# Convolution taps in a two-block transformer kernel: ScalarE's tap products added by accumulating DMA transfers in place of Pool additions

## The chip, the cores and the metric

The kernel runs on one core of a Trainium2 chip. The metric is the time of one execution on the device in microseconds (us). The engines are called PE (TensorE, matrix products; PEld are its weight loads), DVE (VectorE), ACT (ScalarE), POOL (GpSimd) and SP (SyncE, which issues the transfers between DRAM and the on-chip memory SBUF). Each engine works through its own queue of instructions in order and waits on semaphores for the others.

## The reference

The input is a sequence of 1024 tokens with 1024 features. Two blocks follow one another. The first has three branches (a recurrent one of RWKV type, a convolution and an attention to a memory of 256 rows) that are gated, added, projected and added to the input. The second has two layers with gated scans and differential attention. The change lies in the convolution of the first block:

```
u = glu_in[..., :1024] * sigmoid(glu_in[..., 1024:])
u = conv_general_dilated(u, w_dw[:, None, :], (1,), [(30, 0)],
        feature_group_count=1024) + b_dw        # 31 taps per feature, causal
u = silu(layernorm(u)) * silu(conv_gate)
y_conv = u @ w_proj_conv + b_proj_conv
```

Each of the 1024 features has 31 weights of its own: the result at time t is the sum of `w[j] * u[t - 30 + j]` over j from 0 to 30, plus a bias.

## The kernel before, in words

Features lie on the 128 partitions, in eight tiles, and time along the rows. The convolution is done by element-wise work in 16 groups, one for each tile of features `i` and half of the time `h` (512 columns). A group is the generator `taps` (line 567 in the print below). It loads `u` with 30 columns of the past (lines 574 and 577) and shares the 31 taps out. ACT starts the accumulator `acc` with tap 0 and the bias (line 581). DVE adds taps 1 to 14 to `acc`, each by one instruction that multiplies and adds (line 589). The last 16 taps (`GT = 16`) are multiplied by ACT (line 585): the first product goes straight into a second sum, `acg`, the other 15 into a tile `ut`, of which there are two buffers, and POOL adds each to `acg` (line 587, through the helper `tt`, whose instruction has line 211 in the profile). At the end DVE adds `acg` to `acc` (line 592), and the sum is stored to DRAM as `uc` (line 593). `acc`, `acg` and `u` have one buffer each, so a group starts when the one before it has let go of them.

The groups run inside the recurrent branch (`rwkv`), beside two other kinds of work. PE's order there is the written order (`pinned`): 16 units of 24 steps, with a step of the recurrence (`unit_chain`: `S`, `Z`, `SA`), a piece of the matrices for the next unit (`unit_gram`, whose short DVE recurrence writes `B`, `tm` and `T`), some of the preparation (`unit_prep`: `AR`, `BK`), and then a burst of dense matmuls `ps` (`project`) that cover the waits of the recurrence. In two of three steps `next_tap` moves the current group of taps by one tap of ACT, one of POOL and one of DVE. The dense matmuls take weights split into a high and a low half; ACT writes the high half `whi`, and the low half `wlo` is a subtraction on DVE or, for the second four row blocks of a weight tile in this stretch (`wlo_g`), on POOL.

`keep` in `taps` ties an instruction of ACT or DVE behind the instruction that was traced before it on the same engine. All else on ACT, DVE, POOL and SP is ordered by a planner that simulates the program; the additions on POOL and the last addition of a group are not tied. Semaphores are placed by the framework: a transfer that writes `acg` waits for the last one that wrote it, and a product that writes a `ut` buffer waits for the last reader of that buffer.

Of the kernel before, what the change touches and what calls it, by code (L numbers as in the profile page):

```python
# [14 lines left out]
ALU = mybir.AluOpType  # L15
# [166 lines left out]
class Kern:  # L182
# [18 lines left out]
    def keep(self, ins):  # L201

        if self.strict:
            self.tc.keep_in_program_order(ins)
# [362 lines left out]
    def taps(self, i, h):  # L567

        nc, p1 = self.nc, self.r1
        u = p1.tile([128, 542], F32, tag="uh", name="uh")  # L570
        src = self.D[f"u{i}"]
        if h == 0:
            nc.gpsimd.memset(u[:, 0:30], 0.0)
            nc.sync.dma_start(out=u[:, 30:542], in_=src[:, 0:512])
            self.spill(f"uc{i}")
        else:
            nc.sync.dma_start(out=u, in_=src[:, 482:1024])
        keep = self.tc.keep_in_program_order
        w = lambda j: self.V("w_dw", 31 * i + j)
        acc, acg = (p1.tile([128, 512], F32, tag=t, name=t) for t in ("uacc", "uacg"))  # L580
        keep(nc.scalar.activation(out=acc, in_=u[:, 0:512], func=AF.Identity, scale=w(0), bias=self.V("b_dw", i)))  # L581
        for k in range(GT):
            j = 31 - GT + k
            t = acg if k == 0 else p1.tile([128, 512], F32, tag="ut", name="ut", bufs=2)
            keep(nc.scalar.activation(out=t, in_=u[:, j:j + 512], func=AF.Copy, scale=w(j)))  # L585
            if k:
                self.tt(acg, acg, t, ALU.add, eng=nc.gpsimd)
            if 1 <= k <= 30 - GT:
                keep(nc.vector.scalar_tensor_tensor(out=acc, in0=u[:, k:k + 512], scalar=w(k), in1=acc, op0=ALU.mult, op1=ALU.add))  # L589
            if k:  # L590
                yield False
        self.tt(acc, acc, acg, ALU.add)
        nc.sync.dma_start(out=self.D[f"uc{i}"][:, h * 512:h * 512 + 512], in_=acc)
# [1271 lines left out]
```

## Time and profile before

| | before |
|---|---|
| median of 3 runs | 3795.87 us (3791.98 to 3798.04) |
| profiled execution | 3792.68 us |
| its span, first to last instruction | 3790.8 us |
| PE busy in the span | 3511.8 us, 93% |
| DVE busy | 2309.6 us, 61% |
| ACT busy | 1847.6 us, 49% |
| POOL busy | 863.9 us, 23% |
| mean granted TensorE clock | 0.970 |

Busy time is the time in which an engine had an instruction in work; a busy PE is not PE at its peak, since its matmuls overlap. Times inside a profile count from the first instruction. An engine's idle time is put down to what ended it, as the semaphores tell it.

### The profile page before, as it was taken

How to read it: one execution, taken by the hardware profiler on the slowest of the kernel's cores; microseconds unless marked ns; L12 is line 12 of the kernel's file. 1: busy time of each engine (PE TensorE's matmuls, PEld its weight loads, DVE VectorE, ACT ScalarE, POOL GpSimd, SP SyncE). 2: the span in 40 equal slices, each digit the busy share in tenths (PEclk: the TensorE clock that was granted, in tenths of full speed). 3: DMA queues.
4: the chain of work that ended last, by engine and by line, in shares of the span. 5: the costliest groups of instructions: out<-in, count | busy, mean ns of one | idle time of the engine just before them, and what ended most of it. 6: DMA issues, size and time to landing. Idle time of an engine off the chain costs nothing.

```text
span 3790.8 us, 69648 instructions
## 1 busy us (share of the span) xinstructions
PE 3511.8 (93%) x27522; PEld 2762.9 (73%) x27522; DVE 2309.6 (61%) x4461; ACT 1847.6 (49%) x3281; POOL 863.9 (23%) x738
## 2 busy tenths in 40 slices
PE   7999999999989999999999999989899999898997
PEld 5877766766766667766778867767798667677886
DVE  4345777777777767655554463567495545774873
ACT  4333444444444444435343344575485444754762
POOL 1002333332333233343022320002222300022221
PEclk9999999999999999999999999999999999999998
DMA  4421222222222222225644444234531342344513
GB/s 146 151 91 58 89 77 75 80 80 80 80 75 83 77 83 95 76 100 184 227 156 155 138 155 149 80 118 150 168 103 56 130 146 85 115 130 149 153 42 109
DMA packets 234039, 426.09 MB, mean 112 GB/s; under 512 B 26352, under 2 KB 45808, under 8 KB 233584
## 3 DMA queue, kind: packets, MB, share of 16 engines
q1 hardware_dynamic: 233712, 421.64, 34.2%
q8 instruction: 216, 3.54, 0.4%
q14 instruction: 111, 0.91, 0.1%
HBM read 287.32 MB, written 134.22 MB: 111 GB/s over the span
## 4 chain that ended last, share of the span: by engine, by line
PE 64%; DVE 18%; DMA 6%; ACT 6%; issue 5%; POOL 1%; SPq 0%; DVEq 0%; POOLq 0%; ACTq 0%
PE ps L259 44%; PE sc L259 3%; PE o_ps L259 3%; PE tps L259 2%; PE ch L259 2%; DVE uacc L589 2%; PE g L259 1%; PE wt L262 1%; DVE tm L211 1%; DVE T L211 1%; PE aps L259 1%; DVE h L211 1%; DMA raw<-d_x 1%; DVE t L217 1%; DVE B L806 1%
## 5 line engine op out<-in xcount | busy, mean ns | idle before, releaser
L259 PE MATMUL ps<-hh,whi 128*128 128x512 f32 (+2 forms) x3056 | 1282.8, 420 | 42.7 <-DVE st L211 21.6
L259 PE MATMUL ps<-hh,wlo 128*128 128x512 f32 (+2 forms) x3056 | 1203.5, 394 | 5.2 <-DVE wlo L211 5.1
L259 PE MATMUL ps<-hl,whi 128*128 128x512 f32 (+2 forms) x3056 | 1203.3, 394 | 2.4 <-DVE hl L211 2.3
L259 PEld LDWEIGHTS ps<-hh,whi 128*128 128x128 f32 (+1 forms) x3056 | 584.3, 191 | 209.7 <-issue 29.3
L259 PEld LDWEIGHTS ps<-hh,wlo 128*128 128x128 f32 (+1 forms) x3056 | 584.3, 191 | 138.6 <-DVE wlo L211 6.6
L259 PEld LDWEIGHTS ps<-hl,whi 128*128 128x128 f32 (+1 forms) x3056 | 585.5, 192 | 128.7 <-issue 18.1
L208 ACT ACTIVATE whi<-wraw 128x512 fp32r<-128x512 f32 x486 | 303.4, 625 | 530.4 <-PE ps L259 408.6
L211 DVE TENSOR_TENSOR wlo<-wraw,whi 128x512 fp32r<-128x512 f32 x398 | 292.2, 736 | 386.2 <-ACT whi L208 346.8
L211 POOL TENSOR_TENSOR uacg<-uacg,ut 128x512 f32<-128x512 f32 x240 | 338.5, 1410 | 785.1 <-ACT ut L585 642.9
L211 POOL TENSOR_TENSOR st<-st,rope 128x512 f32<-128x512 f32 x64 | 93.4, 1480 | 892.0 <-DVE st L427 566.1
L208 ACT ACTIVATE st<-ps 128x512 f32<-128x512 f32 (+2 forms) x260 | 149.2, 574 | 214.6 <-PE ps L259 182.7
L589 DVE SCALAR_TENSOR_TENSOR uacc<-uh,vecs,uacc 128x512 f32<-128x512 f32 x224 | 207.6, 927 | 7.9 <-ACT uacc L581 6.9
L211 POOL TENSOR_TENSOR wlo<-wraw,whi 128x512 fp32r<-128x512 f32 x88 | 121.2, 1377 | 283.9 <-ACT whi L208 261.3
L211 POOL TENSOR_TENSOR acc<-acc,sq 128x512 f32<-128x512 f32 (+1 forms) x91 | 124.4, 1375 | 253.8 <-ACT sq L208 252.2
L585 ACT ACTIVATE ut<-uh,vecs 128x512 f32<-128x512 f32 x240 | 166.0, 715 | 4.4 <-POOL uacg L211 3.7
L1414 DVE TENSOR_REDUCE D<-sc 128x1 f32<-128x1024 f32 x128 | 153.9, 1219 | 13.6 <-PE sc L259 13.2
L208 ACT ACTIVATE p<-sc,D 128x1024 f32<-128x1024 f32 x128 | 142.5, 1114 | 24.5 <-DVE D L1414 23.4
L259 PE MATMUL o_ps<-h,wT 128*128 128x128 f32 x1024 | 125.3, 275 | 2.0 <-ACT wT L208 2.0
L259 PEld LDWEIGHTS o_ps<-h,wT 128*128 128x128 f32 x1024 | 122.0, 192 | 6.9 <-ACT wT L208 3.9
L259 PE MATMUL ps<-oh,wlo 128*128 128x512 f32 x256 | 103.3, 403 | 4.6 <-DVE wlo L211 4.6
L211 DVE TENSOR_TENSOR h<-h,tot 128x512 f32<-128x512 f32 x120 | 79.7, 701 | 42.0 <-ACT kk L208 36.4
L259 PE MATMUL ps<-oh,whi 128*128 128x512 f32 x256 | 105.1, 411 | 0.0
(333 smaller groups left out, 5773.5 us busy)
## 6 DMA issues: line engine op xcount, KB each, us to landing
wraw<-in_w_in_dram SPq DMA_DIRECT2D x326, 256.0 KB, 2.8
wraw<-in_w_out_dram SPq DMA_DIRECT2D x76, 256.0 KB, 2.7
g<-st SPq DMA_DIRECT2D x48, 256.0 KB, 2.4
y<-st SPq DMA_DIRECT2D x48, 256.0 KB, 2.0
gt<-y SPq DMA_DIRECT2D x48, 256.0 KB, 3.1
wraw<-in_w_mem_kv_dram SPq DMA_DIRECT2D x32, 256.0 KB, 2.9
yp<-gt SPq DMA_DIRECT2D x32, 256.0 KB, 3.3
yt<-yp SPq DMA_DIRECT2D x32, 256.0 KB, 3.1
```

The source lines that it names most:

```text
L208: self.keep(self.nc.scalar.activation(out=out, in_=in_, func=func, **kw))
L211: self.keep((eng or self.nc.vector).tensor_tensor(out=out, in0=a, in1=b, op=op))
L217: self.keep(self.nc.vector.scalar_tensor_tensor(out=out, in0=a, scalar=s, in1=b, op0=op0, op1=op1))
L259: self.pin(self.nc.tensor.matmul(out, lhsT=lhsT, rhs=rhs, start=start, stop=stop))
L262: self.pin(self.nc.tensor.transpose(out, in_, self.C("ident")))
L585: keep(nc.scalar.activation(out=t, in_=u[:, j:j + 512], func=AF.Copy, scale=w(j)))
L589: keep(nc.vector.scalar_tensor_tensor(out=acc, in0=u[:, k:k + 512], scalar=w(k), in1=acc, op0=ALU.mult, op1=ALU.add))
L806: nc.vector.stream_shuffle(out=B[:, :, 0:w], in_=N16[:, :, s + 1:16], mask=[s] * 16 + [16 + s] * 16)
L1414: self.keep(nc.vector.reduce_max(out=D(b)[:, c:c + 1], in_=sc[b, c], axis=AX.X, negate=True))
```

## The change

One line of `taps` changes. The 15 additions of a group that POOL computes become 15 transfers that POOL issues. A transfer reads the product `ut` and the sum `acg` from SBUF, adds them on the way and writes `acg`. The buffers, the products on ACT, the multiply-adds on DVE and the order of the loop stay.

```
             keep(nc.scalar.activation(out=t, in_=u[:, j:j + 512], func=AF.Copy, scale=w(j)))
             if k:
-                self.tt(acg, acg, t, ALU.add, eng=nc.gpsimd)
+                nc.gpsimd.dma_start(out=acg, in_=t, accum_op=ALU.add)
             if 1 <= k <= 30 - GT:
```

## Rows read from the trace of the kernel before

**Rows 1.** The page: busy time of the engines, and POOL's share in 40 slices (tenths).
```profile
PE 3511.8 (93%) x27522; PEld 2762.9 (73%) x27522; DVE 2309.6 (61%) x4461; ACT 1847.6 (49%) x3281; POOL 863.9 (23%) x738
...
POOL 1002333332333233343022320002222300022221
```
**Rows 2.** Windows, 300 to 1670 us: length, busy us of five engines, clock, DMA share, GB/s.
```profile
300.00:1670.00 1370.00, 1276.44 (x10964) 947.73 (x10964) 968.03 (x2349) 647.14 (x1195) 438.59 (x321) 0.98 0.24 79
```
**Rows 3.** The page's groups, POOL: busy us, mean ns of one | idle before, releaser.
```profile
L211 POOL TENSOR_TENSOR uacg<-uacg,ut 128x512 f32<-128x512 f32 x240 | 338.5, 1410 | 785.1 <-ACT ut L585 642.9
...
L211 POOL TENSOR_TENSOR wlo<-wraw,whi 128x512 fp32r<-128x512 f32 x88 | 121.2, 1377 | 283.9 <-ACT whi L208 261.3
```
**Rows 4.** Waits of PE, 300 to 1670 us: us in total, times, longest.
```profile
PE ch L259 <- DVE S L217: 46.4, 24, 5.6
PE ch L259 <- DVE Z L211: 21.2, 19, 3.5
PE vps L259 <- DVE bv L211: 13.6, 14, 2.2
PE ch L259 <- ACT SA L208: 5.6, 8, 2.3
```
**Rows 5.** Timeline, 442 to 447 us: start, us, engine, line, instruction, idle before it.
```profile
442.34 0.22 DVE L211 TENSOR_TENSOR tm<-B,T 128x72 f32<-128x72 f32 x1
...
442.94 1.47 POOL L211 TENSOR_TENSOR uacg<-uacg,ut 128x512 f32<-128x512 f32 x1 [4.49 <-DVE T L211]
443.20 1.29 DVE L211 TENSOR_TENSOR tm<-B,T 128x64 f32<-128x64 f32 x1
...
446.29 0.21 DVE L211 TENSOR_TENSOR Z<-ch,X 128x64 f32<-128x64 f32 x1
...
446.56 0.33 PE L259 MATMUL ch<-Z,TT 64*64 64x64 f32 x4 [3.04 <-DVE Z L211]
```
**Rows 6.** Groups of DVE by line, 300 to 1670 us: columns as in rows 3.
```profile
L589 DVE SCALAR_TENSOR_TENSOR uacc<-uh,vecs,uacc 128x512 f32<-128x512 f32 x224 | 207.6, 927 | 7.9 <-ACT uacc L581 6.9
L211 DVE TENSOR_TENSOR tm<-B,T 128x120 f32<-128x120 f32 (+14 forms) x225 | 79.0, 351 | 0.4
L211 DVE TENSOR_TENSOR T<-T,tm 128x120 f32<-128x120 f32 (+14 forms) x225 | 75.7, 337 | 4.8
...
L217 DVE SCALAR_TENSOR_TENSOR AR<-kkn,E 128x256 f32<-128x256 f32 x28 | 27.2, 970 | 0.0
```
**Rows 7.** By tile, the same four: ns least/median/most, first and last start (us), forms.
```profile
L589 DVE SCALAR_TENSOR_TENSOR uacc<-uh,vecs,uacc x224: 701/745/1843, 305.2 to 1662.9; 128x512 f32<-128x512 f32 x112
...
L211 DVE TENSOR_TENSOR tm<-B,T x240: 161/218/1337, 254.5 to 1635.3; 128x120 f32<-128x120 f32 x8, 128x104 f32<-128x104 f32 x8, 128x88 f32<-128x88 f32 x8, 128x72 f32<-128x72 f32 x8
L211 DVE TENSOR_TENSOR T<-T,tm x240: 166/225/1354, 254.8 to 1635.5; 128x120 f32<-128x120 f32 x8, 128x104 f32<-128x104 f32 x8, 128x88 f32<-128x88 f32 x8, 128x72 f32<-128x72 f32 x8
...
L217 DVE SCALAR_TENSOR_TENSOR AR<-kkn,E x32: 413/424/1526, 216.7 to 1575.8; 128x256 f32<-128x256 f32 x32
```
**Rows 8.** Transfers: times issued, KB of each, median us from issue to landing.
```profile
wraw<-in_w_in_dram SPq DMA_DIRECT2D x326, 256.0 KB, 2.8
...
uc<-uacc SPq DMA_DIRECT2D x16, 256.0 KB, 2.0
...
hl<-d_y SPq DMA_DIRECT2D x16, 256.0 KB, 6.2
...
h<-s0z SPq DMA_DIRECT2D x4, 512.0 KB, 4.8
```
**Rows 9.** By tile, ACT's products and the first tap: columns as in rows 7.
```profile
L585 ACT ACTIVATE ut<-uh,vecs x240: 704/713/744, 304.9 to 1662.1; 128x512 f32<-128x512 f32 x120
...
L581 ACT ACTIVATE uacc<-uh,vecs x16: 802/815/820, 303.6 to 1596.3; 128x512 f32<-128x512 f32 x16
```
**Rows 10.** Timeline of ACT, 661 to 669 us: columns as in rows 5.
```profile
662.54 1.34 ACT L585 ACTIVATE ut<-uh,vecs 128x512 f32<-128x512 f32 x2
...
666.61 1.32 ACT L585 ACTIVATE ut<-uh,vecs 128x512 f32<-128x512 f32 x2
```

More of the change, by code (lines that the diff above doesn't have):

```diff
@@ L586, in taps @@
             if k:
-                self.tt(acg, acg, t, ALU.add, eng=nc.gpsimd)
+                nc.gpsimd.dma_start(out=acg, in_=t, accum_op=ALU.add)
             if 1 <= k <= 30 - GT:
```

## The prediction

> **What bounds the kernel now.** I read the page's busy shares first, then the windows of the stretch in which the taps run, then what TensorE (PE) waits for there, then VectorE (DVE) and its collisions. PE is busy 93% of the span, and the taps occupy POOL in the slices from the fourth to the eighteenth [rows 1]. Cut to 300 to 1670 us, the stretch with all tap work, PE is busy 1276 of 1370 us, DVE 968, ACT 647, POOL 439 [rows 2]. POOL has two jobs there, the tap additions (240 of them, 338.5 us over the kernel) and a part of the weights' low halves; it waits for ACT more than it works [rows 3]. So POOL is no bound by its hours. PE's idle time shows whose hours count: 46.4 us for DVE's S, 21.2 for Z, 13.6 for bv, and 5.6 for ACT's SA [rows 4]. DVE ends 81 us of PE's waits and ACT nearly none. What I look for is therefore what the change does to DVE, and what could make ACT late enough to matter.
>
> **What the POOL additions do to DVE.** One gap shows it whole. At 442.94 POOL begins an addition of 1.47 us; DVE's product tm that starts at 443.20 takes 1.29 us where the one before it, nearly as wide, took 0.22; DVE then works without a pause to Z at 446.29, and PE, which has waited 3.04 us, goes on at 446.56 [rows 5]. So 1.07 of these 3.04 us, 35%, is DVE standing behind a POOL addition. By groups: the taps' own multiply-adds on DVE last 927 ns in the mean and 745 in the median, 224 of them, 40.8 us too much; tm 351 against 218 (225: 29.9 us), T 337 against 225 (225: 25.2 us), the first AR form 970 against 424 (28: 15.3 us) [rows 6, 7]. The four make 111 us. Each maximum lies about one POOL addition above the minimum (1843 against 701 ns) [rows 7]. The additions are 338.5 of POOL's 439 us, 77% [rows 2, 3], so some 86 of the 111 us are theirs; the low halves stay.
>
> **Part 1, the additions go.** 240 POOL instructions of 1410 ns leave POOL. That itself is worth nothing, since no PE wait names POOL [rows 4]; it is worth what DVE gets back, 86 us in these four groups. What of it reaches PE is bounded by the PE waits that DVE ends, 81 us above and nothing below (the PE order is fixed, and a DVE that is earlier at one step can still meet the next PE instruction late). The gap worked out by hand gives 35% of 81, which is 28 us. I take 40: it lies by that row, and a little above it, since a queue on DVE that is 86 us shorter is also shorter in gaps without a collision of their own.
>
> **Part 2, the transfers come.** Each accumulating transfer is issued from POOL's queue. It needs its product from ACT, and since all add into one tile, each also needs the landing of the one before. Let L be the time from the moment both are there to the landing. The trace has no transfer issued from POOL, none that adds and none from SBUF to SBUF, so L is bounded by rows: 2.0 us is the store of a tile of the same size (uc), 2.8 the load of one (wraw), 4.8 a load of twice the bytes (h from s0z), and 6.2 the slowest group of 256 KB loads (hl) [rows 8]. The adding transfer reads two tiles and writes one, so it moves more than a load and, unlike h, writes only 256 KB. I take 4.0, between 2.8 and 4.8.
>
> By the Trainium skill (DMA: Bandwidth & Descriptors, Anatomy of one DMA — SWDGE (gpsimd) path) a transfer issued from GpSimd costs about 2.0 us plus its bytes at 436 GB/s, by estimate 2.6 us for 256 KB without the second read. By that the two costs of part 3 would nearly vanish and the sum would be 3760; no run so far shows such a transfer.
>
> **Part 3, what waits for the landings.** (a) ACT. A product needs one of two ut buffers, so product k waits for the landing of k-2; before, POOL freed it 1.4 us later. The products come at a mean distance of (1662.1 - 304.9) / 239 = 5.7 us counted without the first of each group [rows 9], but not evenly: at 662.54 and 666.61 us two stand back to back [rows 10]. With L = 4.0 the first pair, ended at 663.25 and 663.88, lands at 667.3 and 671.3; the next two, at 666.6 and 667.2, would wait 0.7 and 4.0 us. The same arithmetic with the starts of all 240 gives 79 us of ACT waits in 33 products (4 us at L = 2.0, 144 at 4.8). Behind the waiting product stand ACT's SA, the weights' high halves and the emptying of PSUM. PE waits 5.6 us for ACT in a stretch in which ACT is idle 723 us [rows 2, 4], so most short delays vanish in that idle time. I charge PE a tenth, 8 us; the bounds are 0 and 79. (b) DVE. The last addition of each of the 16 groups (acc + acg) now needs the last landing, with S, Z and the T recurrence queued behind it. By the same arithmetic it would stand 37 us in all at L = 4.0 (4 at 2.0, 62 at 4.8). DVE is idle 402 us there and PE waits for it 81, a fifth [rows 2, 4]; I charge a third, 12 us, since this wait comes on top of a full queue; bounds 0 and 37. (c) POOL. Its low halves stand behind transfers that wait, by up to L. No PE wait of [rows 4] names a low half; I charge nothing, and if that cover is gone each late one costs at most L, for some 70 of them. (d) The next group's accumulator still waits for the store of uc, which follows (b); that shifts the start of a group by L less 1.4 us, once in 86 us, and ACT has room. (e) 240 x 256 KB more traffic meets DMA engines that are 24% busy [rows 2]; nothing. The instructions of ACT and DVE around the taps are ordered by a planner that will see other durations; I give that no sign.
>
> **The sum.** 40 gained, 8 + 12 paid: 20 us less. The profiled execution took 3792.68 us (span 3790.8 and 1.9 around it), the median of the runs is 3.2 above it. 3792.7 - 20 + 3.2 = 3776 us.
>
> **The rivals.** *Slower, the chain of landings.* A group of taps starts every (1596.3 - 303.6) / 15 = 86.2 us [rows 9]. Within it there are 15 landings one after the other, and at the seam the last addition (0.7), the store (2.0) and three ACT instructions of 0.7 to 0.8 us, some 5 us. The chain fills the period from L = (86.2 - 5) / 15 = 5.4 us. Before that the waits in ACT and DVE already eat the gain: at L = 5.0 the arithmetic gives 167 us on ACT and 71 on DVE, charged as above 17 + 24 = 41, as much as the gain. From L = 5.0 the mechanism decides. At 5.5 it gives 298 and 109 us; the ACT waits then are long, and a quarter of them, 75, reaches PE, with 36 of DVE and 40 gained: 3867. At 6.2 the period is 15 x 6.2 + 5 = 98 us, 12 more, sixteen times: 188 us less the 40, 3944. For it: the mean distance of the products is not far above what L may be, and POOL's own issue comes on top of the landing. Against it: the two rows of the same size, 2.0 and 2.8, are far below 5. *No change.* PE's waits for S and Z are a matter of the fixed order, and only the collisions in the queue just ahead of them count; then the gain is the 20 that the waits cost, and the time is 3796. For it: S itself waits for PE in turn. *No relief for DVE.* If POOL holds DVE up just as long while it issues a transfer as while it adds, the 20 us of cost stand alone: 3816. The rows can't exclude it, as they hold no issue by POOL.
>
> The Trainium skill (SBUF — State Buffer, Who interferes with whom) says that a DVE instruction with two SBUF inputs contends with a GpSimd instruction that reads SBUF and not with one that only writes it, and that descriptor generation needs the write side, which it calls inferred. The first half agrees with the maxima of 1843 and 1354 ns [rows 7], and tm, T and AR all have two inputs in SBUF. By the second the relief is full, so I give this rival little; no row here shows it.
>
> **Chances.** The forecast (3738 to 3788) has 0.47, no change 0.16, the chain of landings 0.28, no relief 0.09. A measurement of this kernel can tell about 0.2%, 7.6 us, from no change. Faster is the forecast, 0.47; the same is 0.16; slower is 0.28 + 0.09 = 0.37. The range begins at 3738, where a gain of 60 (between the 40 and the 81) is hardly paid for, and ends at 3880, a little above the chain at L = 5.5; beyond it lies the rest of that rival.
>
> **What would show it.** In the profile after: the 224 multiply-adds of DVE near 745 ns in the mean, with the remaining excess from the low halves; AR and tm at their medians; DVE some 90 us less busy between 300 and 1670; PE's waits for S, Z and bv down by about half. L shows as the time from a transfer's issue to its landing, near 4 us. ACT's ut should wait some tens of us for landings in all, and the last addition of a group 1 to 3 us. The forecast is wrong if the landings take 5 us or more and ACT's waits for ut reach hundreds of us, or if DVE's mean durations do not fall, or if they fall and PE's waits stay.

## The result, and the profile after

The changed kernel takes 3750.14 us (median of 4 runs, 3747.09 to 3768.94) against 3796.95 for the kernel before (now with four runs); the ratio is 0.9882 [0.9864, 0.9899], which is 45 us less. Forecast were 3776 and 20 us less: the direction and the range hold, the size is off by more than a factor of two. The profiled execution took 3749.38 us with a span of 3747.6.

Windows of the changed kernel from 300 to 1627 us. That is the work that lay between 300 and 1670 before (PE 10962 matmuls against 10964); columns as in [rows 2]:
```profile
300.00:1627.00 1327.00, 1269.47 (x10962) 942.81 (x10960) 825.31 (x2348) 648.44 (x1194) 307.39 (x321) 0.99 0.53 129
```
The stretch is 43 us shorter, and that is the whole difference of the spans: from its end to the last instruction both kernels take 2121 us. DVE is busy 143 us less for the same work, POOL 131 less, ACT as before. PE stands idle for 58 us (1327 less 1269) where it stood for 94.

Waits of PE in the changed kernel, 300 to 1670 us, against [rows 4]:
```profile
PE ch L259 <- DVE Z L211: 14.4, 14, 3.6
PE ch L259 <- DVE S L217: 14.2, 13, 3.3
PE vps L259 <- DVE bv L211: 14.1, 13, 2.2
PE ch L259 <- ACT SA L208: 8.7, 9, 2.2
```
The waits for S and Z went from 68 to 29 us. The one for bv stayed. The one for ACT grew by 3.

DVE's groups in the changed kernel, the same stretch, against [rows 6]:
```profile
L589 DVE SCALAR_TENSOR_TENSOR uacc<-uh,vecs,uacc 128x512 f32<-128x512 f32 x224 | 172.4, 769 | 16.8 <-ACT uacc L581 15.8
L211 DVE TENSOR_TENSOR tm<-B,T 128x120 f32<-128x120 f32 (+14 forms) x225 | 56.1, 249 | 0.4
L211 DVE TENSOR_TENSOR T<-T,tm 128x120 f32<-128x120 f32 (+14 forms) x225 | 55.7, 248 | 4.7
...
L217 DVE SCALAR_TENSOR_TENSOR AR<-kkn,E 128x256 f32<-128x256 f32 x28 | 11.7, 416 | 0.1
```
The means came down to near the medians of [rows 7]: 35 + 23 + 20 + 16 = 94 us in these four groups. The other 49 of the 143 us lie in forms that the prediction did not count. Nearly all of these have both inputs in SBUF: the `BK` made from `av` and `sg` fell from 728 to 417 ns, `n` made from `NM` from 957 to 684, `gS` from 424 to 356. The forms that take an input from PSUM, the memory where PE leaves its results, did not move (`NM` 420 and 421 ns, `Z` 215 and 215, the `bv` made from `bps` 689 and 689).

The new transfers: POOL's issue and the time from its start to the landing, from the tile's view (ns, then us), and two neighbours from POOL's timeline:
```profile
L587 POOL DMA_DIRECT2D uacg<-ut x240: 850/862/1014, 304.9 to 1623.1; - x120
...
DMA to landing us min/median/max: 3.2/3.5/8.0
```
```profile
640.83 0.88 POOL L587 DMA_DIRECT2D uacg<-ut  x1 [8.95 <-ACT whi L208]
...
644.88 0.88 POOL L587 DMA_DIRECT2D uacg<-ut  x1 [1.88 <-DMA uacg<-ut]
```
The second transfer waits for the landing of the first and starts 4.05 us behind it. That is the step of the chain for which the prediction took 4.0; the 142 steps in which a transfer starts within 0.7 us of the landing before it have a median of 4.1. The Trainium skill (DMA: Bandwidth & Descriptors, Anatomy of one DMA — SWDGE (gpsimd) path) gives by estimate 2.6 us for a transfer of this size, setup included; the 3.5 us measured from the start of the issue are 0.9 more, and the measurement decides.

What waits for the landings, from the waits of ACT and of DVE, 300 to 1670 us:
```profile
ACT ut L585 <- DMA uacg<-ut: 92.2, 51, 4.2
...
ACT uacc L581 <- DMA uc<-uacc: 24.3, 10, 4.6
```
```profile
DVE uacc L211 <- DMA uacg<-ut: 40.5, 15, 7.2
```
Foretold were 79 us for ut and 37 for the last additions. So the landing, the waits and DVE's relief in the four groups that were counted are close to the prediction. What was wrong is what PE gains and pays for them, and the experiments price that.

### The profile page after: what moved, and what is told of

Same layout as the page of the kernel before. It is cut to its first block, busy times and chain, and to the rows that moved or that the text cites. A ratio compares the mean times of both kernels' runs of the same rounds, so it can differ in the third digit from the quotient of the medians.

```text
span 3747.6 us, 69779 instructions
## 1 busy us (share of the span) xinstructions
PE 3506.8 (94%) x27522; PEld 2758.5 (74%) x27522; DVE 2166.9 (58%) x4461; ACT 1848.2 (49%) x3281; POOL 732.3 (20%) x738
## 4 chain that ended last, share of the span: by engine, by line
PE 35%; DMA 8%; DVE 6%; ACT 4%; issue 3%; POOL 1%; SPq 0%; DVEq 0%; POOLq 0%; ACTq 0%
PE ps L259 23%; PE sc L259 3%; PE o_ps L259 3%; PE wt L262 1%; DMA raw<-d_x 1%; DVE h L211 1%; DVE t L217 1%; DMA wraw<-in_w_out_dram 1%; PE aps L259 1%; DMA yp<-gt 1%; DVE wlo L211 1%; ACT st L208 1%; POOL st L211 1%; PE ops L259 1%; ACT whi L208 1%
## 5 line engine op out<-in xcount | busy, mean ns | idle before, releaser
L587 POOL DMA_DIRECT2D uacg<-ut x240 | 207.8, 866 | 953.7 <-ACT ut L585 393.0
L585 ACT ACTIVATE ut<-uh,vecs 128x512 f32<-128x512 f32 x240 | 168.7, 717 | 93.1 <-DMA uacg<-ut 92.2
L589 DVE SCALAR_TENSOR_TENSOR uacc<-uh,vecs,uacc 128x512 f32<-128x512 f32 x224 | 172.4, 769 | 16.8 <-ACT uacc L581 15.8
L208 ACT ACTIVATE st<-st 128x512 f32<-128x512 f32 (+1 forms) x96 | 60.2, 627 | 89.0 <-DVE st L211 78.0
```

Source lines behind the costliest of these rows:

```text
L208: self.keep(self.nc.scalar.activation(out=out, in_=in_, func=func, **kw))
L587: nc.gpsimd.dma_start(out=acg, in_=t, accum_op=ALU.add)
```

## The experiments

Three theories stood at first. A: DVE's relief is all of it, and the waits for landings cost PE nothing. B: the waits cost what was charged, and the relief is worth more than was credited. C: the planner's other order of DVE and ACT is what helped. Ratios are to the kernel before on the same chip; a difference of 0.01 is 38 us.

**Without the sum** (e1_no_sum). The products are made and not added.
```
-                nc.gpsimd.dma_start(out=acg, in_=t, accum_op=ALU.add)
```


> Leaves out the sum of ACT's 15 products of a group: the products are still made, neither POOL nor a transfer adds them. So DVE is free of POOL's additions and nobody waits for a landing. Theory A (the gain is DVE's relief and the waits for landings cost PE nothing): as the changed kernel, 3750, within 8 us. Theory B (the waits do cost the 20 us that were charged, and the relief alone is worth some 65): 3730. Theory C (the gain is the planner's other order of DVE and ACT, not the relief): this kernel has a third order, so anywhere from 3740 to 3797.

Measured: 3715.83 us, ratio 0.9776 [0.9761, 0.9791]: 87 us less than before on its chip, 40 less than the change's ratio. A falls, and B is too small on both sides. Windows of this kernel over the same work, and its PE waits:
```profile
300.00:1579.00 1279.00, 1252.97 (x10963) 932.45 (x10963) 817.51 (x2349) 646.63 (x1195) 99.46 (x81) 1.00 0.26 85
```
```profile
PE ch L259 <- DVE S L217: 13.0, 13, 5.0
PE vps L259 <- DVE bv L211: 12.5, 14, 1.4
PE ch L259 <- DVE Z L211: 5.7, 7, 2.5
PE ch L259 <- ACT SA L208: 2.4, 5, 1.1
```
The stretch is 91 us shorter than before. PE's idle time is 26 us in place of 94, which is 68 of them. The other 23 are PE's busy time, 1253 in place of 1276 for the same matmuls, with a granted clock of 1.00 in place of 0.98 (of the full 2.4 GHz). In the trace's record of the granted clock 51 of the 1370 us before are at the lower level, 1.2 GHz, 34 of the 1327 in the changed kernel and none of the 1279 here; work that took 51 us at half the clock takes some 26 less at the full one, near the 23. Each of the twelve falls of the clock before comes during a pause of PE or within 2 us behind one. The PE waits of [rows 4], 81 us, were thus no ceiling for the 91: with its gaps nearly closed PE was also granted more clock.

**Reads or any work of POOL** (e2_reads, e3_writes). Behind each transfer POOL does needless work, which in one kernel reads SBUF and in the other only writes it.
```
+        dum = p1.tile([128, 256], F32, tag="dum", name="dum")
...
                 nc.gpsimd.dma_start(out=acg, in_=t, accum_op=ALU.add)
+                for c in (0, 256):       # e2_reads
+                    self.tt(dum, u[:, c:c + 256], u[:, c + 30:c + 286], ALU.add, eng=nc.gpsimd)
+                for c in range(4):       # e3_writes, in place of these two
+                    nc.gpsimd.memset(dum, 0.0)
```


> The changed kernel, and behind each transfer POOL does an addition of the same 512 columns (two of 256) on data that nobody needs: POOL reads two SBUF tiles again, the sum still goes by transfers. Theory A: DVE's multiply-adds are back at 900 ns or more in the mean and the time is 3785 to 3800. Theory B: the collisions come back and the waits stay, 3800 to 3820. Theory C: the order is the new one, 3750 to 3760.

> The changed kernel, and behind each transfer POOL fills a tile of 256 columns four times: POOL is held up in a like way but reads nothing from SBUF. If the relief is that POOL no longer reads while DVE does: DVE's multiply-adds stay near 770 ns and the time is 3750 to 3760. If any work of POOL beside DVE slows it, or if POOL's free hours are what helps: 3770 to 3800.

Measured: 3821.74 us with reads, ratio 1.0047 [1.0033, 1.0060]; 3769.05 with writes, 0.9908 [0.9894, 0.9922]. DVE's groups by line, 300 to 1720 us, first of the kernel with reads, then of the one with writes:
```profile
L592 DVE SCALAR_TENSOR_TENSOR uacc<-uh,vecs,uacc 128x512 f32<-128x512 f32 x224 | 194.1, 867 | 12.6 <-ACT uacc L582 11.7
L211 DVE TENSOR_TENSOR tm<-B,T 128x120 f32<-128x120 f32 (+14 forms) x225 | 73.0, 325 | 0.5
```
```profile
L592 DVE SCALAR_TENSOR_TENSOR uacc<-uh,vecs,uacc 128x512 f32<-128x512 f32 x224 | 175.7, 784 | 18.1 <-ACT uacc L582 17.1
L211 DVE TENSOR_TENSOR tm<-B,T 128x120 f32<-128x120 f32 (+14 forms) x225 | 54.2, 241 | 0.4
```
Waits of PE and of ACT in the kernel with reads, 300 to 1670 us:
```profile
PE ch L259 <- DVE S L217: 43.3, 25, 5.1
PE ch L259 <- DVE Z L211: 23.3, 17, 2.9
```
```profile
ACT ut L586 <- DMA uacg<-ut: 68.5, 40, 4.8
```
With reads most of the long durations, PE's waits for S and Z and the time come back, 63 us over the changed kernel, although the sum still goes by transfers; so C falls as the main cause. Nor is it that POOL's extra work makes the transfers late: ACT waits less for landings than in the changed kernel, 68.5 us against 92.2. With writes DVE keeps its short instructions and the time rises by 10 us. Theory A's figure for the reads (3785 to 3800) was too low, B's fits within 2 us. The two are not an exact pair: the traced fills took 219 us of POOL, the additions 362. The rule of the Trainium skill that was cited (SBUF — State Buffer, Who interferes with whom) agrees with both means, 867 and 784 ns, against 769 with neither.

**The waits for ut** (e4_ut3).
```
-  ... tag="ut", name="ut", bufs=2)
+  ... tag="ut", name="ut", bufs=3)
-        wup = p2.tile([128, 256], F32, tag="wup", name="wup")
+        wup = p1.tile([128, 256], F32, tag="wup", name="wup")
```


> The changed kernel with three buffers for ut in place of two (and one for wup in place of two, to make room): ACT's waits for landings, 92 us, should fall to under 30. Theory A: within 5 us of 3750. Theory B: a tenth to a quarter of the waits that go, 7 to 20 us faster, 3730 to 3743. Theory C says nothing of it.

Measured: 3739.36 us, ratio 0.9835 [0.9821, 0.9848], 18 us less than the change. ACT's waits for landings in this kernel (300 to 1670 us):
```profile
ACT ut L585 <- DMA uacg<-ut: 21.7, 14, 3.6
```
70 us of ACT's waits less are 18 us of time, a quarter and not the tenth that was charged. For the same work as in the windows above, the profiled execution shows more, 28 us (1299 against 1327):
```profile
300.00:1599.00 1299.00, 1257.32 (x10962) 935.28 (x10961) 826.90 (x2348) 647.13 (x1196) 306.61 (x321) 1.00 0.54 131
```
So the price lies between a quarter and two fifths of the wait. (`wup` has one buffer in this kernel, to make room; no run has that alone.)

**Longer chains** (e5_half, e6_full). A copy that the next transfer has to wait for, behind every other one and behind every one.
```
                 nc.gpsimd.dma_start(out=acg, in_=t, accum_op=ALU.add)
+                if k % 2:                # e6_full: without this line
+                    nc.gpsimd.dma_start(out=t, in_=acg)
```


> The changed kernel, and behind every other accumulating transfer one that copies the sum into ut and that the next one has to wait for: the chain of landings grows from some 3.5 to some 5.2 us per tap in the mean, which is about the distance of the taps. By the charges of the prediction (a tenth of ACT's waits, a third of DVE's) at 5.2 us: 45 us slower than the changed kernel, 3795. Theory A (PE hardly pays for these waits before the chain fills the period): 3750 to 3770.

> The same behind every accumulating transfer: some 7 us per tap, past the period of 86 us for 15 taps. All theories: slower, since the chain then sets the pace: 15 x 7 + 5 = 110 us per group against 86, sixteen times 24 = 380 us, 4130. If the taps can run late behind the recurrent branch without holding ACT, much less: under 3900.

Measured: 3929.34 us, ratio 1.0355 [1.0335, 1.0376], and 4295.93, ratio 1.1320 [1.1297, 1.1343]. Both expectations missed by far, the first by 134 us. Landings in the first, by kind (times issued, KB, median us):
```profile
uacg<-ut POOLq DMA_DIRECT2D x240, 256.0 KB, 3.3
ut<-uacg POOLq DMA_DIRECT2D x128, 256.0 KB, 2.3
```
A group there is a chain of 15 and 8 such transfers, and of all 368 transfers 326 start within 0.7 us of the landing before them, where 142 of 240 did in the changed kernel. The groups start (1698.6 - 303.4) / 15 = 93.0 us apart, against 86.2 before: the chain sets the pace, as the rival had it. Waits of ACT in e5_half (300 to 1700 us), then of PE (300 to 1670):
```profile
ACT ut L585 <- DMA ut<-uacg: 175.9, 62, 6.7
ACT ut L585 <- DMA uacg<-ut: 106.1, 47, 4.8
...
ACT uacc L581 <- DMA uc<-uacc: 60.7, 12, 10.9
```
```profile
PE ch L259 <- ACT SA L208: 48.6, 19, 5.8
PE ch L259 <- DVE Z L211: 47.8, 19, 7.3
```
ACT waits 226 us more for landings and stores than in the changed kernel, and the time is 180 us longer. In this regime the time grows by most of ACT's wait, where with short waits it grew by a quarter to two fifths.

**The last addition as a transfer** (e7_final).
```
-        self.tt(acc, acc, acg, ALU.add)
+        nc.gpsimd.dma_start(out=acc, in_=acg, accum_op=ALU.add)
```


> The changed kernel with the last addition of a group (acc + acg) as an accumulating transfer too: DVE's 40 us of waits for landings go, and 11 us of work. Theory A: no more than 8 us faster, 3742 to 3750. Theory B (a third of DVE's waits reach PE): 12 to 15 us faster, 3735 to 3738.

Measured: 3797.75 us, ratio 0.9999 [0.9984, 1.0014]; a miss, 44 us slower than the change. DVE's wait for the landing is gone, but a second landing now stands between the last product and the store, and ACT's first instruction of the next group waits for that store. Behind it DVE's first multiply-add of the group waits in turn. ACT's wait, DVE's, then PE's (300 to 1670 us):
```profile
ACT uacc L581 <- DMA uc<-uacc: 66.7, 14, 7.3
```
```profile
DVE uacc L589 <- ACT uacc L581: 63.3, 14, 7.0
```
```profile
PE ch L259 <- ACT SA L208: 21.9, 9, 5.5
```
ACT waits 42 us more for the store than in the changed kernel, and DVE did not win its 40 us back: it waits 63 for ACT's first tap, where it waited 16. So both engines stand at the seam, the change from one group to the next. How much of the 44 us each of them costs is not shown.

**More taps on ACT** (e8_gt20).
```
-GT = 16
+GT = 20
...
-                    if (u * STEPS + s) % 3:
+                    if (u * STEPS + s) % 6:
```


> The changed kernel with 20 taps of 31 on ACT and the transfers in place of 16 (and a tap in five of six steps, so that all find a place): DVE does 4 x 16 multiply-adds less, 48 us; the chain has 19 landings per group. If DVE's load is what PE waits for: 10 to 15 us faster than the changed kernel, 3735 to 3740. If the relief was the collisions only and PE's remaining waits are set by the order: 3750. If the chain of landings binds (19 x 3.5 + 5 = 72 us of 86): slower, 3760.

Measured: 3880.70 us, ratio 1.0227 [1.0207, 1.0247]; a miss on all three. DVE has less to do, but ACT's 304 products come closer together than the chain allows. More taps on ACT and more steps with a tap were not run apart. ACT's wait (300 to 1700 us), then PE's (300 to 1670):
```profile
ACT ut L585 <- DMA uacg<-ut: 279.8, 124, 6.5
```
```profile
PE ch L259 <- ACT SA L208: 50.3, 26, 5.4
```

**The seam, and both waits together** (e9_seam, e10_ring). acc is stored after DVE's last tap, and the products' sum is added to it in DRAM.
```
+        acg = p1.tile([128, 512], F32, tag="uacg", name="uacg", bufs=2)
...
+                if k == 30 - GT:
+                    nc.sync.dma_start(out=self.D[f"uc{i}"][:, h * 512:h * 512 + 512], in_=acc)
...
-        self.tt(acc, acc, acg, ALU.add)
-        nc.sync.dma_start(out=self.D[f"uc{i}"][:, h * 512:h * 512 + 512], in_=acc)
+        nc.gpsimd.dma_start(out=self.D[f"uc{i}"][:, h * 512:h * 512 + 512], in_=acg, accum_op=ALU.add)
```
with `wup` in one buffer as in e4_ut3; in e10_ring acg and ut share `tag="ut"` with `bufs=4`.

> The changed kernel with another seam between groups: acc is stored as soon as DVE's last tap is in it, the sum of ACT's products is added to the stored tile in DRAM by one more accumulating transfer, and acg has two buffers (wup one, for room). So no engine waits for the last landing of a group: DVE's 40 us and ACT's 24 us of waits at the seam go, ACT's 92 us for ut stay. Of the 42 us that waits cost in the changed kernel (0.9882 against 0.9776 of the time before without the sum), three ut buffers gave back 19. If the seam holds the rest: 18 to 25 us faster than the changed kernel, ratio 0.982 to 0.984 to before. If the rest is traffic or POOL's time for issuing: within 6 us of the changed kernel, 0.987 to 0.989.

> The same seam, with the two buffers of acg and the two of ut in one ring of four, so that within a group three ut buffers are free. Both waits, for ut and at the seam, should mostly go. If the two are all that the transfers cost: near the kernel without the sum, ratio 0.977 to 0.980. If they overlap or traffic costs something: 0.980 to 0.984.

Measured: 3732.78 us, ratio 0.9834 [0.9813, 0.9855], and 3706.27, ratio 0.9754 [0.9730, 0.9778]. The seam is worth 18 us, and both together 49, where each alone gave 18. For the work of the windows above the profiled execution of e9_seam takes 10 us less than the changed kernel:
```profile
300.00:1617.00 1317.00, 1266.28 (x10962) 940.73 (x10961) 820.41 (x2333) 648.45 (x1196) 322.51 (x336) 0.99 0.55 133
```
e10_ring computes the whole reference and is the fastest of the kernels that do. Its windows over the same work, and ACT's waits for landings (300 to 1670 us):
```profile
300.00:1582.00 1282.00, 1254.47 (x10968) 933.62 (x10967) 819.52 (x2333) 647.76 (x1196) 321.77 (x336) 1.00 0.57 137
```
```profile
ACT ut L586 <- DMA uacg<-ut: 19.9, 14, 4.5
```
In this stretch it stands where the kernel without the sum stands: 1282 us against 1279, PE idle 28 against 26, clock 1.00. In the profiled executions it is ahead only behind the stretch, where the two kernels have the same work.

**Issuing and traffic alone** (e11_traffic). To the kernel without the sum, behind each of ACT's products:
```
+            if k:
+                nc.gpsimd.dma_start(out=self.spill(f"junk{k % 4}")[:, 0:512], in_=u[:, 0:512])
```


> The kernel without the sum of ACT's products, with 240 transfers issued from POOL that copy 512 columns of u to scratch tiles in DRAM and that no computation waits for (four scratch tiles in turn; u's reload still waits for the last of them): POOL's time for issuing and about the same bytes on the DMA engines, without the waits for landings. If issuing and traffic are free: 0.977 to 0.979, as without the sum. If they hold a part of the 42 us: 0.980 to 0.988.

Measured: 3723.86 us, ratio 0.9800 [0.9785, 0.9816], 9 us more than without the sum (0.9776). The intervals overlap, so a cost of a few us is likely and not certain; the work of the windows takes 1287 us in the profiled execution, against 1279.

## Why the prediction was right in its direction and wrong in its size

The steps, by the prediction's own parts. *What bounds the kernel*: right. The reads behind e2_reads and e3_writes show that it is POOL's additions on DVE that PE waited for. *Part 1, DVE's hours*: right for the four groups, 86 us foretold and 94 measured, and low for all of DVE, some 90 foretold and 143 measured. *Part 1, what reaches PE*: this is the step that failed. "I take 40", bounded by "81 us above"; without the sum it is 87 us. Two errors made it small. The share of 35% came from one gap, and in fact 68 of PE's 94 idle us went, 72%. (One gap shows only the collision inside it, and not the queue on DVE that earlier ones left; that this is the reason is argued and was not traced through other gaps.) And the bound took PE's waits as all that PE can win, while 23 us more came out of PE's busy time at a granted clock of 1.00 instead of 0.98. *Part 2, the landing*: right, 4.05 us per step of the chain where 4.0 was taken. *Part 3, the waits*: 92 and 40.5 us measured, 79 and 37 foretold, from starts that the planner has since moved; *their price*: 20 charged, some 40 paid (0.9882 less 0.9776). By the runs' times it is a quarter of ACT's waits for ut (18 us for the 70 that e4_ut3 removed, so about 24 for all 92), 18 us for the seam where 12 were charged for DVE alone and nothing for ACT's wait for the store (24.3 us, 7.1 before), and perhaps 9 for issuing and traffic where nothing was charged. These add up to 51 and the difference to 40, so they overlap, or the planner's orders or the part behind the taps differ by as much. How the price divides is thus not settled; that it is about twice the 20 is.

So the gain was 87 and not 40, the cost 40 and not 20, and the two errors partly hid each other: that 3750 lies in the range is in part luck. Of the rivals, no change is refuted by the result and by e1_no_sum, and no relief by DVE's means in the changed kernel (769 ns against 927) and by e2_reads. The chain of landings is real but decides later than at the measured step of 4.05: it had about the right period (e5_half fills it) and too low a price. That ACT's idle hours hide the landings holds for a part of the waits only, and for that while single waits stay short.

Not settled: how much of the 10 us between the changed kernel and e3_writes is POOL's time and how much a new order, and which part of e7_final's loss is ACT's and which DVE's.

Nor is the part behind the stretch the same everywhere, though the change does not touch it. Up to the last instruction it takes 2121 us before and after, 2135 in e4_ut3, 2114 in e9_seam, and in the kernel without the sum, then in e10_ring:
```profile
1579.00:3725.20 2146.20, 1979.40 (x14996) 1605.37 (x14994) 1216.12 (x1860) 1083.14 (x1879) 402.08 (x395) 0.95 0.41 130
```
```profile
1582.00:3692.90 2110.90, 1960.33 (x14997) 1588.31 (x14995) 1211.48 (x1860) 1083.32 (x1879) 406.42 (x396) 0.97 0.42 133
```
Of these 35 us, 19 are PE's busy time, at a mean granted clock of 0.95 and 0.97. Why it differs there was not tried. Differences of 10 to 20 us between two kernels may thus come from there in part, and the prices of 18, 18 and 9 us are no firmer than that. The 91 us of the kernel without the sum, counted in the stretch alone, do not depend on it.

## What to carry to other kernels

Compare the mean of a VectorE form with its median before looking at waits: a mean 180 ns above the median, with maxima 1100 ns above the minimum beside GpSimd instructions of 1400, was worth more time here than all of PE's visible waits for that engine. A sum of PE's waits was no ceiling on the gain here. A serial chain of accumulating transfers was cheap here only while it left room in its period and nothing in an in-order queue waited for it: one more buffer and a seam that no engine waits at gave back as much again as the change itself.

## What the runs showed of the hardware that was not expected

An accumulating transfer of 256 KB from SBUF into SBUF costs POOL 0.86 us to issue and lands 3.5 us after its start. A plain copy of the same size between the same tiles lands after 2.3 us (e5_half), beside 3.3 for the accumulating ones of that kernel. Into DRAM an accumulating transfer of 256 KB lands after 4.7 us (e9_seam). POOL filling SBUF beside DVE hardly slows it (784 against 769 ns for the multiply-adds), POOL reading does (867). Between the kernels before and after, DVE's forms with both inputs in SBUF became shorter (`gS` 424 to 356 ns, `n` 957 to 684), and those with an input from PSUM did not (`NM` 420 and 421, `Z` 215 and 215). With PE's idle time in this stretch at 94, 58 and 26 us its granted clock was 0.98, 0.99 and 1.00, and the same matmuls took 1276, 1269 and 1253 us of PE's busy time (kernel before, changed kernel, kernel without the sum).
